# SwiGLU input projections with seven quarter-block products per pair of tiles

## The chip, the cores and the metric

The kernel runs on one core of a Trainium2 chip. The metric is the device time of one execution in microseconds (us); the profile gives the span of one profiled execution and, within it, every instruction.

## The reference

One inference step of a two-layer decoder trunk in float32, for 512 prompt tokens and 8 sample tokens that share the weights (520 columns in all, model width 1024). Layer 0 mixes tokens by a gated MLP over chunks, layer 1 by a gated delta rule. Each mixer is followed by the part that changes here:

```python
def rmsnorm(x, g):
    xf = x * lax.rsqrt(jnp.mean(x * x, axis=-1, keepdims=True) + EPS)
    return xf * g

def swiglu_ffn(h, w_in, w_out):
    gate, up = jnp.split(h @ w_in, 2, axis=-1)      # 1024 -> 2 x 2816
    return (jax.nn.silu(gate) * up) @ w_out         # 2816 -> 1024

x = x + swiglu_ffn(rmsnorm(x, norm_ffn[i]), ffn_w_in[i], ffn_w_out[i])
```

## The kernel before, in words

Activations lie with features on the 128 partitions: x is 8 tiles (k) of 128 features by 520 tokens. Every float32 product is made of three matmuls on rounded parts: weights and activations are split into a high part (a cast on ScalarE, `S`) and a low part (a subtraction on VectorE, `V`, or GpSimd, `G`), and `products` (L162) issues high x high, high x low and low x high for each k. `HALF` cuts the tokens in two, 256 and 264 columns; one half tile of output is 8 x 3 = 24 matmuls into one PSUM bank. Weights come from memory by SP's queue, 512 KB for an output tile (`load_raw`, L126), and are split by `split_w` (L133).

`ffn` (L418) runs over the 22 tiles of the inner width in chunks of 8, 8 and 6. For each tile it makes the gate product in two half tiles, multiplies it by the norm factor of each token (`norm.scaled`, L238), applies Silu, multiplies by the factor again on GpSimd (L430), makes the up product in two half tiles, multiplies (L436) and splits the result (`split_act`, L172) as input of the projection. Behind each chunk `out_proj` (L273) runs 8 tiles x 2 halves over it and adds to x. Its last `tail` tiles take first one half and then the other.

The norm does not hold up the products: `Feed` (L241) splits x times gain as soon as a tile of x is there, while `Norm` (L177) adds up squares. `finish` (L213) puts two steps behind later half tiles, by `after` (L148): `reduce` (column sums on TensorE, the reciprocal root in nine small VectorE operations, a diagonal) and `spread` (the factor brought to all partitions by TensorE, copied by ScalarE, L230).

The order is set by the program text, by pools of buffers (three raw weights, three split ones, three banks for products), and by a compile-time scheduler that may pull an instruction ahead where another waits; `pin` keeps some in program order. In layer 1 the new states of the samples (L1016) are laid between the products by `after`: a load, and three counts later one GpSimd operation of 128x512 (L1028) and four on VectorE (L1030).

## Time and profile before

| what | value |
|---|---|
| time, median of 3 runs | 1501.12 us (1499.31 to 1503.87) |
| profiled execution: span | 1499.8 us (no time around it is given) |
| instructions | 29605, of which 12192 matmuls |
| TensorE, weight loads | 97%, 95% busy |
| VectorE, ScalarE, GpSimd | 54%, 36%, 29% busy |
| moved by DMA | 155.69 MB, mean 104 GB/s |
| chain that ended last, by engine | PE 85%, DVE 11%, ACT 2% |

The chain is followed back from the last instruction: at each step to what released it, or to the instruction before it on its engine. A group of instructions is a line of the kernel with its operation and tiles (in and out, partitions x elements), its count, its total and mean time, and the idle time of the engine before it. PE is TensorE, PEld its weight loads, DVE VectorE, ACT ScalarE, POOL GpSimd, SP the engine whose queue issues the loads.

### The profile page before, as it was taken

Reading aid. Unit: us, or ns where it says so; the run is one execution under the profiler, and the core shown is the slowest. Engines: PE = TensorE matmul, PEld = TensorE weight load, DVE = VectorE, ACT = ScalarE, POOL = GpSimd, SP = SyncE. Lnnn points to the kernel's source line nnn. Section 1 sums busy time; section 2 is a strip of 40 time slices with the busy share of each in tenths; the row PEclk is TensorE's granted clock in tenths of the full one; section 3 lists DMA queues with packets and bytes.
Section 4 is the critical chain, followed back from the end, with each engine's and each line's share of the span. In section 5 each row is a group of like instructions: output and inputs, shape, how many; then the busy total and the mean of one; then the engine's idle time right before and its main releaser. Section 6 shows DMA issues by size and latency. Waiting matters only on the chain.

```text
span 1499.8 us, 29605 instructions
## 1 busy us (share of the span) xinstructions
PE 1447.5 (97%) x12192; PEld 1429.8 (95%) x12192; DVE 813.3 (54%) x1727; ACT 540.6 (36%) x1067; POOL 440.7 (29%) x468
## 2 busy tenths in 40 slices
PE   8999999999999999998788899999999999999997
PEld 8999999999999999998788888999999999999997
DVE  7447445553333333347777988686754344444344
ACT  5445323433312321334643255434433313321333
POOL 2113102333302320336444212311334412430333
PEclk9999999999999999999899999999999999999999
DMA  6222222322322232224311224234423443444331
GB/s 205 81 85 87 86 85 85 101 85 88 97 89 95 88 96 90 94 82 144 104 58 71 79 79 134 87 103 146 150 85 107 141 148 120 124 143 134 114 95 68
DMA packets 79367, 155.69 MB, mean 104 GB/s; under 512 B 10848, under 2 KB 41216, under 8 KB 79232
## 3 DMA queue, kind: packets, MB, share of 16 engines
q1 hardware_dynamic: 78944, 153.27, 31.1%
q8 instruction: 96, 1.57, 0.4%
q10 hardware_dynamic: 288, 0.52, 0.1%
q14 instruction: 39, 0.32, 0.1%
HBM read 142.18 MB, written 11.59 MB: 103 GB/s over the span
## 4 chain that ended last, share of the span: by engine, by line
PE 85%; DVE 11%; ACT 2%; issue 2%; DMA 1%; POOL 0%; SPq 0%; ACTq 0%; DVEq 0%; POOLq 0%
PE mm L168 76%; DVE kcs L579 1%; PE ax L406 1%; DVE sc L677 1%; DVE inv L678 1%; PE ax L867 1%; DVE t L579 1%; DVE sqacc L196 1%; PE ax L334 1%; DVE rs_u L118 1%; PE ax L643 1%; DVE inv L670 1%; PE sx L819 1%; PE sx L826 0%; PE ax L227 0%
## 5 line engine op out<-in xcount | busy, mean ns | idle before, releaser
L168 PE MATMUL mm<-hfh,wsp 128*128 128x256 f32 (+1 forms) x2816 | 510.4, 283 | 0.0
L168 PEld LDWEIGHTS mm<-hfh,wsp 128*128 128x128 f32 x2816 | 436.0, 189 | 0.1
L168 PE MATMUL mm<-hfl,wsp 128*128 128x256 f32 (+1 forms) x1408 | 398.8, 283 | 0.0
L138 ACT CAST wsp<-raw 128x1024 fp32r<-128x1024 f32 (+2 forms) x225 | 231.8, 1030 | 456.3 <-PE mm L168 408.5
L139 DVE TENSOR_TENSOR wsp<-raw,wsp 128x1024 fp32r<-128x1024 f32 (+2 forms) x193 | 234.0, 1213 | 91.4 <-ACT wsp L138 90.8
L168 PEld LDWEIGHTS mm<-hfl,wsp 128*128 128x128 f32 x1408 | 265.8, 189 | 0.0
L168 PE MATMUL mm<-fmh,wsp 128*128 128x264 f32 (+1 forms) x1408 | 254.9, 283 | 0.0
L168 PEld LDWEIGHTS mm<-fmh,wsp 128*128 128x128 f32 x1408 | 217.6, 188 | 0.0
L168 PE MATMUL mm<-hbh,wsp 128*128 128x264 f32 (+1 forms) x1024 | 203.9, 295 | 7.8 <-DVE t L574 5.7
L168 PE MATMUL mm<-hnh,wsp 128*128 128x264 f32 (+1 forms) x1024 | 197.9, 287 | 2.9 <-POOL wsp L139 1.0
L168 PE MATMUL mm<-fml,wsp 128*128 128x264 f32 (+1 forms) x704 | 198.9, 283 | 0.0
L430 POOL TENSOR_TENSOR t<-t,rbc 128x256 f32<-128x256 f32 x88 | 95.3, 1083 | 315.9 <-ACT t L429 315.9
L168 PEld LDWEIGHTS mm<-hbh,wsp 128*128 128x128 f32 x1024 | 166.8, 196 | 9.7 <-DVE t L574 6.3
L238 DVE TENSOR_TENSOR t<-mm,rbc 128x264 f32<-128x264 f32 (+1 forms) x160 | 68.4, 428 | 193.6 <-PE mm L168 192.1
L168 PEld LDWEIGHTS mm<-hnh,wsp 128*128 128x128 f32 x1024 | 161.5, 189 | 4.0 <-POOL wsp L139 1.2
L168 PE MATMUL mm<-hbl,wsp 128*128 128x264 f32 (+1 forms) x512 | 150.0, 293 | 0.0
L168 PE MATMUL mm<-hnl,wsp 128*128 128x256 f32 (+1 forms) x512 | 145.6, 285 | 0.4 <-DVE hnl L261 0.4
L175 POOL TENSOR_TENSOR fml<-t,fmh 128x256 fp32r<-128x256 f32 x88 | 95.9, 1089 | 150.0 <-ACT fmh L174 150.0
L168 PEld LDWEIGHTS mm<-fml,wsp 128*128 128x128 f32 x704 | 132.6, 188 | 0.0
L282 DVE TENSOR_TENSOR x<-mm,x 128x264 f32<-128x264 f32 (+1 forms) x128 | 54.5, 426 | 124.9 <-PE mm L168 124.5
L436 DVE TENSOR_TENSOR t<-mm,t 128x256 f32<-128x256 f32 x88 | 37.7, 429 | 119.2 <-PE mm L168 117.0
L168 PEld LDWEIGHTS mm<-hbl,wsp 128*128 128x128 f32 x512 | 100.3, 196 | 0.3
(331 smaller groups left out, 1989.9 us busy)
## 6 DMA issues: line engine op xcount, KB each, us to landing
raw<-in_f_w_in SPq DMA_DIRECT2D x88, 512.0 KB, 3.2
raw<-in_f_w_out SPq DMA_DIRECT2D x32, 512.0 KB, 3.5
raw<-in_b_w_in SPq DMA_DIRECT2D x32, 512.0 KB, 3.3
raw<-in_a_w_in SPq DMA_DIRECT2D x31, 512.0 KB, 3.2
raw<-in_a_w_out SPq DMA_DIRECT2D x16, 512.0 KB, 3.6
raw<-in_f_w_out SPq DMA_DIRECT2D x16, 384.0 KB, 3.1
L<-rows_d SPq DMA_DIRECT2D x16, 256.0 KB, 3.6
t<-in_st_delta SPq DMA_DIRECT2D x16, 256.0 KB, 3.2
```

Of the source, the lines that this page charges most:

```text
L118: V.tensor_tensor(u, u, s, ALU.mult)
L138: S.copy(hi, r)
L139: (eng or V).tensor_tensor(w[:, 1, i:i + n, :], r, hi.bitcast(F32), ALU.subtract)
L168: PE.matmul(ps[:, :n], lhsT=w[:, a, k, :], rhs=act[b][:, k, c0:c0 + n], start=(i == 0), stop=(i == last))
L175: (eng or G).tensor_tensor(act[1][:, k, c0:c0 + n], tmp, hi.bitcast(F32), ALU.subtract)
L196: (eng or G).tensor_tensor(a, a, t, ALU.add)
L238: V.tensor_tensor(t, ps[:, :n], self.r[:, c0:c0 + n], ALU.mult)
L282: V.tensor_tensor(dst, ps[:, :w], (xin(j)[:, c0:c0 + w] if xin else dst), ALU.add)
L334: PE.transpose(ps[:, j * P:(j + 1) * P], vf[j][:, c * C:(c + 1) * C], ident)
L430: G.tensor_tensor(s, s, norm.r[:, c0:c0 + nn], ALU.mult)
L436: V.tensor_tensor(sg[h], ps[:, :nn], sg[h], ALU.mult)
L579: V.scalar_tensor_tensor(y[:, :T], raw[:, j:j + T], wc[:, n, j:j + 1], y[:, :T], ALU.mult, ALU.add)
```

## The change

The input projections of SwiGLU are computed on blocks. An operand block is half of the features (4 tiles k) by half of the tokens (260 columns); a weight block is half of the features by one output tile, and two neighbouring output tiles make a two by two arrangement. Instead of eight products of blocks, seven are made, of sums and differences of blocks (`Seven`): the weight sums are four 128x512 operations on GpSimd for each pair of tiles (`load`), seven blocks of weights are split in four steps (`split`), and seven steps of 12 matmuls add into three banks; ScalarE copies intermediate sums out of PSUM, and VectorE combines them with the last ones (`step`). The activation sums are made once per layer (`quarter`). For this, activations are multiplied by gain and norm factor before they are split (`Scaled`), and the two multiplications behind the gate product go. The first pair of gate tiles and of up tiles in a layer is still made by half tiles; each later pair has one group of seven for gates and one for ups, their steps interleaved by the sorted list `plan` (one unit is one step of either). The projection of a chunk stands in that list too, and takes the other set of banks. Buffers: five raw weights and four split ones. The tail of `out_proj` grows from two tiles to three in both mixers' last projections and in layer 0's SwiGLU. The small weights of the next mixer are loaded at the end of layer 0's SwiGLU, not ahead of it; the samples' new states come every 10 counts, not 7, a count being a half tile or a step. The diff's core:

```diff
...
-    wraw = ctx.enter_context(tc.tile_pool(name="wraw", bufs=3))
-    wspl = ctx.enter_context(tc.tile_pool(name="wspl", bufs=3))
+    wraw = ctx.enter_context(tc.tile_pool(name="wraw", bufs=5))
+    wspl = ctx.enter_context(tc.tile_pool(name="wspl", bufs=4))
...
+        def finish(self, h, at=1, then=None):
+                if then:
+                    then()
...
+    class Scaled:
+        def __init__(self, x, gain, regions, sums, name):
+            self.x, self.gain, self.regions, self.sums, self.name = x, gain, regions, sums, name
+            self.act = None
+        def __call__(self, k, h, eng=None):
+            if self.act is None:
+                self.act = act_pair(*self.regions, self.name)
+                self.norm = Norm()
+            self.norm.add(self.x, k, h, V if k >= 6 else eng)
+            if k == KD - 1:
+                self.norm.finish(h, 1, lambda: self.half(h))
+        def half(self, h):
+            c0, n = HALF[h]
+            if not h:
+                self.work = region(7, [P, 4160], "work")
+            y = self.work.rearrange("p (k t) -> p k t", k=KD)
+            for k in range(KD):
+                a = y[:, k, c0:c0 + n]
+                V.scalar_tensor_tensor(a, self.x[:, k, c0:c0 + n], self.gain[:, k:k + 1], self.norm.r[:, c0:c0 + n], ALU.mult, ALU.mult)
+                split_act(a, self.act, k, c0, n, G if k % 2 else V)
+            if h:
+                self.q = tuple(region(i, [P, 4, HK, HT], self.name + "q", F32R) for i in self.sums)
+                after(2, lambda: self.quarter(y, 0))
+                after(3, lambda: self.quarter(y, 2))
+        def quarter(self, y, k):
+            def of(k0, h):
+                return y[:, k0 + k:k0 + k + 2, h * HT:(h + 1) * HT]
+            def two():
+                return t2()[:, :2 * HT].rearrange("p (k t) -> p k t", k=2)
+            def put(i, t, eng):
+                hi = self.q[0][:, i, k:k + 2, :]
+                S.copy(hi, t)
+                eng.tensor_tensor(self.q[1][:, i, k:k + 2, :], t, hi.bitcast(F32), ALU.subtract)
+            s1, s2, s3, s4 = two(), two(), two(), two()
+            V.tensor_tensor(s1, of(0, 1), of(HK, 1), ALU.subtract)
+            V.tensor_tensor(s2, s1, of(0, 0), ALU.subtract)
+            G.tensor_tensor(s3, of(0, 0), of(0, 1), ALU.subtract)
+            V.tensor_tensor(s4, s2, of(HK, 0), ALU.add)
+            for i, (t, eng) in enumerate(((s1, V), (s2, G), (s3, V), (s4, G))):
+                put(i, t, eng)
+        def operand(self, i, b, k):
+            plain = {0: (0, 0), 3: (HK, 0), 6: (HK, 1)}
+            if i in plain:
+                k0, h = plain[i]
+                return self.act[b][:, k0 + k, h * HT:(h + 1) * HT]
+            return self.q[b][:, {1: 0, 2: 1, 4: 2, 5: 3}[i], k, :]
+    class Seven:
+        def __init__(self, feed, src, bank, done, slot):
+            self.feed, self.src, self.bank, self.take, self.slot = feed, src, bank, done, slot
+            self.w, self.banks = {}, {}
+        def load(self):
+            f = self.feed
+            self.raw = [load_raw(a, KD) for a in self.src]
+            o = 2048 * self.slot
+            b11, b21 = (self.raw[0][:, k:k + HK, :] for k in (0, HK))
+            b12, b22 = (self.raw[1][:, k:k + HK, :] for k in (0, HK))
+            t = [f.work[:, o + 512 * i:o + 512 * i + 512].rearrange("p (k n) -> p k n", k=HK) for i in range(4)]
+            G.tensor_tensor(t[0], b11, b12, ALU.add)
+            G.tensor_tensor(t[1], t[0], b22, ALU.add)
+            G.tensor_tensor(t[2], b12, b22, ALU.add)
+            G.tensor_tensor(t[3], t[1], b21, ALU.add)
+            self.parts = (b11, t[0], t[1], b21, t[2], b22, t[3])
+        def split(self, j):
+            w = wspl.tile([P, 2, 2, HK, P], F32R, tag="wsp", name=nm("wsp"))
+            for e, i in enumerate(range(2 * j, min(2 * j + 2, 7))):
+                r, hi = self.parts[i], w[:, 0, e]
+                S.copy(hi, r)
+                V.tensor_tensor(w[:, 1, e], r, hi.bitcast(F32), ALU.subtract)
+                self.w[i] = (w[:, 0, e], w[:, 1, e])
+        def step(self, i):
+            fresh, at = i in (0, 1, 3), "acabaca"[i]
+            if fresh:
+                self.banks[at] = self.bank()
+            ps = self.banks[at]
+            if i == 0:
+                self.kept = t2()
+            w = self.w.pop(i)
+            n, last = 0, 3 * HK - 1
+            for k in range(HK):
+                for a, b in ((0, 0), (0, 1), (1, 0)):
+                    PE.matmul(ps[:, :HT], lhsT=w[a][:, k, :], rhs=self.feed.operand(i, b, k), start=fresh and n == 0, stop=n == last, skip_group_check=not fresh)
+                    n += 1
+            if i == 0:
+                S.copy(self.kept[:, :HT], ps[:, :HT])
+            elif i == 1:
+                S.copy(self.kept[:, HT:TT], ps[:, :HT])
+            elif i == 2:
+                self.kept2 = t1()[:, :HT]
+                S.copy(self.kept2, ps[:, :HT])
+            elif i == 3:
+                self.take(0, 0, lambda t: V.tensor_tensor(t, ps[:, :HT], self.kept[:, :HT], ALU.add))
+            elif i == 4:
+                self.take(1, 1, lambda t: V.tensor_tensor(t, self.kept[:, HT:TT], ps[:, :HT], ALU.subtract))
+            elif i == 5:
+                self.take(1, 0, lambda t: V.tensor_tensor(t, ps[:, :HT], self.kept2, ALU.subtract))
+            else:
+                self.take(0, 1, None, ps[:, :HT])
+            tick()
-    def out_proj(w_out, k0, nk, act, x, xin=None, then=None, early=((), ()), halves=(0, 1), tail=2):
+    def out_proj(w_out, k0, nk, act, x, xin=None, then=None, early=((), ()), halves=(0, 1), tail=2, bank=None):
-            ps = mm3(ws[j], nk, act, h) if h or j not in first else first[j]
+            ps = mm3(ws[j], nk, act, h, bank) if h or j not in first else first[j]
...
-    feed = Feed(x, gffn[:, 0], (1, 2), "hf")
+    feed = Scaled(x, gffn[:, 0], (1, 2), (5, 6), "hf")
...
-        out_proj(a_w_out, half * 8, 8, mid, x, then=feed if half else None)
-    def ffn(layer, x, feed, then):
+        out_proj(a_w_out, half * 8, 8, mid, x, then=feed if half else None, tail=2 + half)
+    def ffn(layer, x, feed, then, final=None):
+        mids = {}
+        def mid(n):
+            c = n // 8
+            if c not in mids:
+                mids[c] = act_pair(3, 4, "fm")
+            return mids[c]
+        hf = feed.act
+        sg = [t2(), t2()]
+        ws = [weights(w_in[n]) for n in (0, 1)]
+        ups = []
+        for h in range(2):
+            c0, nn = HALF[h]
+            for j in range(2):
+                ps = mm3(ws[j], KD, hf, h)
+                S.activation(sg[j][:, c0:c0 + nn], ps[:, :nn], AF.Silu)
+            for j in range(2):
+                if not h:
+                    ups.append(weights(w_in[NF + j]))
+                ps = mm3(ups[j], KD, hf, h)
+                t = t1()[:, :nn]
+                V.tensor_tensor(t, ps[:, :nn], sg[j][:, c0:c0 + nn], ALU.mult)
+                split_act(t, mid(0), j, c0, nn)
+        def project(c):
+            k0, nk = 8 * c, min(8, NF - 8 * c)
+            end = k0 + nk == NF
+            if end and final:
+                final()
+            out_proj(w_out, k0, nk, mids[c], x, then=then if end else None, halves=(layer, 1 - layer), tail=3, bank=None if end else axps)
+        plan = []
+        for p in range(NF // 2 - 1):
+            n = 2 * p + 2
+            gates = {}
+            def gate(j, h, get, ps=None, gates=gates):
+                if not gates:
+                    gates.update({0: t2(), 1: t2()})
+                g = gates[j][:, h * HT:(h + 1) * HT]
+                if get:
+                    get(g)
+                S.activation(g, g if get else ps, AF.Silu)
+            def up(j, h, get, ps=None, gates=gates, n=n):
+                g, t = gates[j][:, h * HT:(h + 1) * HT], t1()[:, :HT]
+                if get:
+                    get(t)
+                    V.tensor_tensor(t, t, g, ALU.mult)
+                else:
+                    V.tensor_tensor(t, ps, g, ALU.mult)
+                split_act(t, mid(n + j), (n + j) % 8, h * HT, HT)
+            for q, (o, bank, take) in enumerate(((0, mmps, gate), (NF, axps, up))):
+                at = 14 * p + 7 * q
+                seven = Seven(feed, [w_in[o + n + j] for j in range(2)], bank, take, q)
+                plan.append((at - 6.2, seven.load))
+                for j in range(4):
+                    plan.append((at + 4 * j - 4.5, lambda seven=seven, j=j: seven.split(j)))
+                for i in range(7):
+                    plan.append((at + 2 * i, lambda seven=seven, i=i: seven.step(i)))
+            if n % 8 == 6 or n + 2 == NF:
+                plan.append((14 * p + (20.2 if n + 2 < NF else 20), lambda c=n // 8: project(c)))
+        for _, event in sorted(plan, key=lambda e: e[0]):
+            event()
...
+    wbas = []
+    def load_ba():
+        wba = region(5, [P, 2, 8, P], "wba", F32R)
+        rba = region(6, [P, 8, 16], "rba")
+        G.memset(wba.bitcast(F32), 0.0)
+        nc.sync.dma_start(rba, b_w_ba)
+        S.copy(wba[:, 0, :, 0:16], rba)
+        V.tensor_tensor(wba[:, 1, :, 0:16], rba, wba[:, 0, :, 0:16].bitcast(F32), ALU.subtract)
+        wbas.append(wba)
+    ffn(0, x, feed, feed_b, load_ba)
+    wba = wbas[0]
...
-    feed = Feed(x, gffn[:, 1], (5, 6), "hf")
-    out_proj(b_w_out, 0, 8, ob, x, xin=xin, then=feed, early=(wo, first))
+    feed = Scaled(x, gffn[:, 1], (5, 6), (1, 2), "hf")
+    out_proj(b_w_out, 0, 8, ob, x, xin=xin, then=feed, early=(wo, first), tail=3)
...
-            new_states(hd, i, 10 + 7 * (2 * hd + i))
+            new_states(hd, i, 12 + 10 * (2 * hd + i))
...
-    nc = _bacc.Bacc("TRN2", target_bir_lowering=False, num_devices=1)
+    nc = _bacc.Bacc("TRN2", target_bir_lowering=False, num_devices=1, dynamic_dma_scratch_size=64)
...
```

## Rows read from the trace of the kernel before

**Rows 1.** The page's parts 1 and 2: engines over the span, TensorE in 40 slices

```profile
PE 1447.5 (97%) x12192; PEld 1429.8 (95%) x12192; DVE 813.3 (54%) x1727; ACT 540.6 (36%) x1067; POOL 440.7 (29%) x468
PE   8999999999999999998788899999999999999997
```

**Rows 2.** The chain that ended last, window 300 to 720 us: start, us, what

```profile
324.98 365.84 PE mm L168 x3048
```

**Rows 3.** TensorE's timeline at layer 0's SwiGLU; its waits from 1060 us on

```profile
317.13 0.68 PE L227 MATMUL ax<-t,ones 128*128 128x128 f32 x4 [1.94 <-DVE t L221]
...
PE ax L227 <- DVE t L221: 1.9, 1, 1.9
```

**Rows 4.** GpSimd: L1028 alone (ns min/median/max), then groups by shape

```profile
L1028 POOL TENSOR_TENSOR sc<-sc,smb x16: 1043/1050/1578, 1144.3 to 1445.3; 128x512 f32<-128x512 f32 x16
...
L430 POOL TENSOR_TENSOR t<-t,rbc 128x264 f32<-128x264 f32 x44 | 62.9, 1430 | 109.5 <-ACT t L429 109.5
L430 POOL TENSOR_TENSOR t<-t,rbc 128x256 f32<-128x256 f32 x44 | 32.4, 736 | 206.4 <-ACT t L429 206.4
```

**Rows 5.** VectorE's groups by shape

```profile
L139 DVE TENSOR_TENSOR wsp<-raw,wsp 128x1024 fp32r<-128x1024 f32 x179 | 221.2, 1236 | 85.6 <-ACT wsp L138 85.1
L436 DVE TENSOR_TENSOR t<-mm,t 128x264 f32<-128x264 f32 x44 | 19.0, 432 | 95.0 <-PE mm L168 95.0
...
L413 DVE TENSOR_TENSOR t<-t,t 128x264 f32<-128x264 f32 x16 | 6.8, 427 | 0.0
L940 DVE TENSOR_TENSOR obl<-t,obh 128x512 fp32r<-128x512 f32 x8 | 5.4, 684 | 0.3 <-ACT obh L939 0.3
```

**Rows 6.** ScalarE's groups by shape

```profile
L138 ACT CAST wsp<-raw 128x1024 fp32r<-128x1024 f32 x207 | 217.2, 1049 | 436.5 <-PE mm L168 396.3 <-issue 31.7 <-ACT t L192 3.6
...
L174 ACT CAST fmh<-t 128x264 fp32r<-128x264 f32 x44 | 18.0, 408 | 0.9 <-DVE t L436 0.9
...
L939 ACT CAST obh<-t 128x512 fp32r<-128x512 f32 x8 | 4.9, 618 | 13.3 <-DVE t L937 13.3
...
L230 ACT COPY rbc<-ax 128x264 f32<-128x264 f32 x5 | 1.9, 378 | 13.7 <-PE ax L227 13.7
```

**Rows 7.** Timelines of VectorE, then GpSimd, 270 to 325 us

```profile
277.20 0.49 DVE L261 SCALAR_TENSOR_TENSOR hfl<-x,gffn,hfh 128x264 fp32r<-128x264 f32 x1
...
293.32 2.33 DVE L261 SCALAR_TENSOR_TENSOR hfl<-x,gffn,hfh 128x264 fp32r<-128x264 f32 x1 [1.11 <-ACT hfh L260]
295.57 0.41 DVE L282 TENSOR_TENSOR x<-mm,x 128x256 f32<-128x256 f32 x1
...
308.07 0.48 DVE L261 SCALAR_TENSOR_TENSOR hfl<-x,gffn,hfh 128x256 fp32r<-128x256 f32 x1 [0.58 <-ACT hfh L260]
308.48 0.42 DVE L196 TENSOR_TENSOR sqacc<-sqacc,t 128x256 f32<-128x256 f32 x1
...
313.01 2.39 DVE L118 TENSOR_TENSOR rs_u<-rs_u,nrm_s 128x3 f32<-128x3 f32 x1
...
292.95 2.40 POOL L139 TENSOR_TENSOR wsp<-raw,wsp 128x1024 fp32r<-128x1024 f32 x1 [1.61 <-ACT wsp L138]
295.30 0.95 POOL L196 TENSOR_TENSOR sqacc<-sqacc,t 128x264 f32<-128x264 f32 x1
```

**Rows 8.** VectorE, line L238: count, ns min/median/max

```profile
L238 DVE TENSOR_TENSOR t<-mm,rbc x160: 403/426/434, 44.6 to 1447.5; 128x256 f32<-128x256 f32 x80, 128x264 f32<-128x264 f32 x80
```

**Rows 9.** VectorE's timeline in layer 1, one new state

```profile
1185.73 1.14 DVE L1030 SCALAR_TENSOR_TENSOR sc<-sc,kqs,sc 128x128 f32<-128x128 f32 x4 [1.66 <-POOL sc L1028]
```

**Rows 10.** VectorE's timeline, second root of layer 0, first and last operation

```profile
321.16 0.16 DVE L208 TENSOR_SCALAR nrm_s<-ax 128x2 f32<-128x2 f32 x1 [1.41 <-PE ax L205]
...
323.19 0.61 DVE L221 TENSOR_SCALAR t<-ident,rs_y 128x128 f32<-128x128 f32 x3
```

**Rows 11.** The page's part 6, DMA issues

```profile
raw<-in_f_w_in SPq DMA_DIRECT2D x88, 512.0 KB, 3.2
```

**Rows 12.** Stretches: us, busy of PE, PEld, DVE, ACT, POOL (x), clock, DMA

```profile
1125.00:1210.00 85.00, 85.00 (x711) 85.00 (x710) 35.76 (x62) 24.57 (x42) 35.08 (x32) 1.00 0.40 125
```

More of the change, by code (lines that the diff above doesn't have):

```diff
@@ L150, in after, with tick @@
         steps.setdefault(done[0] + n, []).append(step)
-    def mm3(w, nk, act, h):
-        ps = products(w, nk, act, h)
+    def tick():
         done[0] += 1
@@ L156, in mm3 @@
             step()
+    def mm3(w, nk, act, h, bank=None):
+        ps = products(w, nk, act, h, bank)
+        tick()
         return ps
@@ L160, in pin, with products @@
         tc.keep_in_program_order(ins)
-    def products(w, nk, act, h):
+    def products(w, nk, act, h, bank=None):
         c0, n = HALF[h]
-        ps = mmps()
+        ps = (bank or mmps)()
         i, last = 0, 3 * nk - 1
@@ L414, in trunk @@
                 split_act(m[:, :nn], mid, k, c0, nn)
-        out_proj(a_w_out, half * 8, 8, mid, x, then=feed if half else None)
-    def ffn(layer, x, feed, then):
+        out_proj(a_w_out, half * 8, 8, mid, x, then=feed if half else None, tail=2 + half)
+    def ffn(layer, x, feed, then, final=None):
         w_in, w_out = f_w_in[layer], f_w_out[layer]
-        hf, norm = feed.act, feed.norm
-        for c0f, nk in ((0, 8), (8, 8), (16, 6)):
-            mid = act_pair(3, 4, "fm")
-            for k in range(nk):
-                wg = weights(w_in[c0f + k], eng=G if c0f + k == 0 else V)
-                sg = []
-                for h in range(2):
-                    c0, nn = HALF[h]
-                    s = norm.scaled(mm3(wg, KD, hf, h), h)
-                    S.activation(s, s, AF.Silu)
-                    G.tensor_tensor(s, s, norm.r[:, c0:c0 + nn], ALU.mult)
-                    sg.append(s)
-                wu = weights(w_in[NF + c0f + k], eng=G if c0f + k == 0 else V)
-                for h in range(2):
-                    c0, nn = HALF[h]
-                    ps = mm3(wu, KD, hf, h)
-                    V.tensor_tensor(sg[h], ps[:, :nn], sg[h], ALU.mult)
-                    split_act(sg[h], mid, k, c0, nn)
-            out_proj(w_out, c0f, nk, mid, x, then=then if c0f == 16 else None, halves=(layer, 1 - layer), tail=2 + layer)
```

11 lines of the change are left out of this document (3 added, 8 removed).

## The prediction

> **What bounds the kernel now.** I read the page's busy times first, then the chain of waits, then the waits of each engine. TensorE is busy 97% of the span, and in the 40 slices it falls below nine tenths only at the start, around the middle mixer and at the end [rows 1]. The chain shows why no other engine matters in the SwiGLU stages: from 324.98 us on it consists of 3048 matmuls in 365.84 us and nothing else, 0.120 us each [rows 2]. So there a matmul that goes away is worth 0.120 us, as long as whatever replaces it stays hidden. TensorE waits only at the two entrances of SwiGLU, 1.9 us each, for the small multiplications behind the norm factor [rows 3]. ScalarE and GpSimd are free for two thirds of the span or so and VectorE for almost half, but that is an average; the question is what they can do together inside the changed stretch.
>
> The profiled execution has a span of 1499.8 us; the page gives no time around it. That is 1.3 us under the median 1501.1 of the runs, whose own spread is 4.6. I count changes against the span and put the result beside the median. Below 0.3% (4.5 us) a measurement of this kernel can't tell a change from none.
>
> **Matmuls removed.** A pair of output tiles took 2 x 2 half tiles of 24 matmuls, 96. It now takes seven products of 4 x 3 matmuls of 260 columns, 84. The first pair of gates and of ups in each layer stays as it was; the other 10 pairs of each go in 40 groups of seven: 40 x 12 = 480 matmuls. The 0.120 us is the mean of 256 and 264 columns, and 260 lies between: **-57.6 us**. Per pair of groups (one of gates, one of ups, interleaved) TensorE needs 168 x 0.120 = 20.2 us where it needed 23.0.
>
> The Trainium skill (TensorE: Matmul & The Clock Gate, section Back-to-back issue gap) gives N/2.4 + 2.5 ns for a warm matmul alone, 110.8 ns at 260 columns; an estimate from it would make the saving 53.2 us. The rows' 120 ns is larger, so the measurement decides.
>
> **What a pair of groups costs the other engines.** GpSimd: eight sums of weight blocks, 128x512. The nearest operation of this shape takes 1.05 us in the median; the four low parts of activations take 0.74 each when undisturbed [rows 4]. Sum 8 x 1.05 + 4 x 0.74 = 11.4 us; the multiplication by the norm factor on GpSimd (88 operations, 95 us in all [rows 4]) goes. VectorE: 14 low parts of weights at 0.684 (128x512), seven reads of PSUM at 0.43, three products in SBUF at 0.43: 9.6 + 3.0 + 1.3 = 13.9 us [rows 5]. ScalarE: 14 casts at 0.62, six copies out of PSUM at 0.38, four casts at 0.41 and four Silu taken as these: 14.3 us [rows 6]. Each alone fits under 20.2, with ScalarE and VectorE at 70%.
>
> **The shared resource.** VectorE and GpSimd do not run side by side when VectorE reads two operands in SBUF. At 292.95 GpSimd starts an operation of 2.40 us, and a VectorE operation that starts 0.37 later takes 2.33 in place of 0.49, ending 0.30 behind it; then GpSimd's next one ends 0.60 behind VectorE. A VectorE operation that reads PSUM passes in 0.41 meanwhile. Even the three-column step of the reciprocal root waits 2.39 [rows 7]. VectorE's reads of PSUM are never lengthened: 434 ns at most in 160 [rows 8]. So what matters is the sum of both engines' time on the shared path. With fixed parts overlapped, a VectorE operation holds it for about its columns over 0.95 per ns (0.30 at 264), and GpSimd 0.14 less than its own time: 14 x 0.56 + 3 x 0.30 + 8 x 0.91 + 4 x 0.60 = **18.4 us** of 20.2. With nothing overlapped it is 9.6 + 1.3 + 11.4 = **22.3 us**. The two ends lie on either side of TensorE's 20.2. Split weights are asked for 4.5 steps ahead of use (6.5 us, a step being 1.44), so a delay of 2 to 3 us is absorbed, and the projection between chunks (16 x 24 x 0.12 = 46 us, almost without GpSimd) lets a backlog drain. I am nearer to the tight end, since in rows 7 both engines hand over without a gap, and take 0.5 us of stall per pair of groups in layer 0: **+5 us** (bounds 0 to 33).
>
> In layer 1 the new states of the samples run in between, now every 10 counts, about 1.4 per pair of groups: each 1.05 on GpSimd [rows 4] and 1.14 on VectorE for four [rows 9], both on the shared path, +2.7 to 3.1 us. That gives 21 to 25 against 20.2. I take 1.5 us of stall per pair: **+15 us** (bounds 0 to 62).
>
> The Trainium skill (GPSIMD Engine Reference, section 4.1 Engine selection) sends two-input elementwise work to VectorE and calls GpSimd about 2x slower. Here 1.05 stands against 0.684, 1.5x; at the page's 2x a block sum would be 1.37 us, by estimate, and the shared path 24.8 with nothing overlapped, more than the 23.0 of before. The measured 1.05 decides, and the change then stays on the right side.
>
> **The entrance.** Before, products started on x times gain while the norm factor was still being made. Now each half waits for it. With T the end of the last first-half product of the mixer's projection (whose tail grows from two tiles to three): x, square and sum about T+1.5; the column sums go behind the next half tile, T+2.9; root and diagonal take 2.6 us [rows 10], T+5.9; the spread stands behind the second, and the factor is in SBUF at T+6.8. Then VectorE scales eight tiles (0.41 each, back to back [rows 7]), subtracts four low parts and GpSimd four (0.60 each on the shared path), beside two evacuations: 7 to 8 us, so T+14.5, when TensorE is free at T+9.2. The first tile takes in k by k, and would have ended at T+12.1: about 3 us of stall. The second half has two more tiles of cover: 0.5. Then the quarter sums: ten operations of 520 columns on VectorE and six on GpSimd, about 12 us on the shared path; the weight sums of the first group use the same region and queue behind the last read of it on GpSimd. TensorE has 12 us of first-pair products to cover it: I take 2. Sum 5.5 per layer, **+11 us** (bounds 2 to 24); the two waits of 1.9 that stood there go into the longer tail: **-3.8**.
>
> **Smaller edits.** Splits for the next groups hold two of the four buffers while the projection of a chunk runs, but its tail wants three, so two products must move ahead of it; the bound is 0 to 2.7 us (a cast and a subtraction, 1.05 + 1.24 and handovers [rows 5]) at four places; I take 0.5: +2. At the last chunk the final low part on GpSimd is needed about 1.8 us after its product: 1 us each: +2. Loads: the same blocks, 3.2 us to landing [rows 11], asked for two at a time over five buffers and thus several steps ahead on SP's queue; if that cover went, 3 us per pair. The moved memset and load of the small weights have 35 us of projection over them: nothing; uncovered they would cost some 4 us once.
>
> **Sum:** -57.6 + 5 + 15 + 11 - 3.8 + 4 = -26.4, so 1473.4 for the span and **1474.7** beside the median.
>
> **Rivals.** (a) TensorE paces everything: the shared path stays at its tight 18.4, and even new states are absorbed by the projections. For it: GpSimd and VectorE together are busy 71 of 85 us in the stretch of layer 1 already, without a TensorE wait [rows 12]. -57.6 + 2 to 11 - 3.8 + 2: 1444 to 1453. Chance 0.10. (b) The shared path paces: 1.5 us of stall in layer 0 and 3.2 in layer 1 per pair, 47 in all: -57.6 + 47 + 11 - 3.8 + 4 = +0.6, 1490 to 1508. For it: the untightened 22.3 and the ScalarE queue, which waits in order for GpSimd's sums and holds up evacuations. Chance 0.18. (c) Slower: VectorE waits out a GpSimd operation at almost every turn, as in [rows 7]. A pair then costs VectorE's own 13.9 plus GpSimd's held 9.7, 23.6 us, and 26.5 in layer 1; 3.4 x 10 + 6.3 x 10 = 97, less about 4 us per chunk that slack takes up (24): +73. -57.6 + 73 + 11.2 = +27: 1528 (1508 to 1545). It decides from about 2.3 us of stall per pair, where the sum crosses zero. Against it: VectorE's reads of PSUM, a fifth of its time, overlap with GpSimd. Chance 0.17.
>
> The Trainium skill (SBUF — State Buffer, section SBUF: two separate sides) says that the loser of this pair blocks for the whole instruction. That is the mechanism of (c), and rows 7 agree (2.33 us in place of 0.49); it gives no rate for the hand-over.
>
> That fewer products run than stated is no rival: the counts are fixed by the loops.
>
> **How the numbers follow.** Forecast 0.55, 1453 to 1490, centre 1474.7. Faster by over 0.3%: 0.55 + 0.10 + 0.08 of (b). Within 0.3%: 0.08. Slower: 0.17 + 0.02. The range reaches over (b) and most of (a): 1447 to 1508, leaving out (c) and a little of (a).
>
> **What would show it.** Matmuls 480 fewer, at 0.120 us apart. GpSimd's block sums at 1.05 alone and near 1.6 behind VectorE; the weight subtractions spread from 0.68 to 1.6. TensorE idle before products of group steps, released by VectorE's weight parts, few in layer 0, more in layer 1; and 3 to 6 us at each entrance, released by the scaled activations. It is wrong if TensorE waits for evacuations or loads, if the entrances cost over 12 us each, or if layer 0 stalls as much as layer 1.

## The result and the profile after

The changed kernel takes 1555.41 us (median of 4 runs, 1554.48 to 1557.60) where the kernel before took 1502.43 on the same chip: a ratio of 1.0363 (95% interval 1.0345 to 1.0382). It is slower by 53 us, against a forecast of 26 us faster. The profiled execution of it has a span of 1553.6 us, 53.8 more than before.

The page's part 1 (busy time, share, instructions) and the first line of its part 4 (the chain that ended last, by engine) show that the matmuls did go and that TensorE now waits:

```profile
PE 1427.6 (92%) x11712; PEld 1392.4 (90%) x11712; DVE 1050.3 (68%) x1999; ACT 648.9 (42%) x1402; POOL 590.2 (38%) x564
...
PE 55%; DVE 30%; ACT 6%; issue 5%; POOL 3%; DMA 1%; SPq 0%; ACTq 0%; DVEq 0%; POOLq 0%
```

There are 480 matmuls fewer than in [rows 1], as counted. But TensorE falls from 97% to 92% of the span, and the chain's share of VectorE rises from 11% to 30%. Stage by stage, from first matmuls on the timeline: SwiGLU of layer 0 lasts 411.6 us (before 396.7), the second mixer 392.7 (389.2), SwiGLU of layer 1 to the end 433.3 (396.3), the start 1.5 less; in all +53.8. The two SwiGLU stages also lost 57.6 us of matmuls, so some 110 us of new waiting came in.

TensorE's waits (total us, times, longest), from the second down; the first lies in the second mixer (L808, 20.0 us, before 14.2):

```profile
...
PE mm L375 <- DVE t L567: 14.7, 2, 7.3
PE ax L173 <- ACT wsp L140: 14.1, 8, 2.7
PE ax L375 <- DVE wsp L361: 10.2, 4, 4.6
PE mm L375 <- ACT t L378: 9.0, 2, 4.5
PE mm L375 <- DVE t L387: 8.7, 8, 2.0
PE ax L232 <- DVE t L226: 6.3, 3, 4.1
```

L567 is the reading of a bank of the first, plain pair of tiles; L378 and L387 are reads of a group's banks; L361 is a group's weight part on VectorE; L140 is the split of a projection's first weight. None of these waits is on a load. The two 1.9 us waits of [rows 3] are gone.

By stretches (us, busy of PE, PEld, DVE, ACT, POOL with counts, granted clock, DMA): the entrance of layer 0, its later groups, and two stretches of groups of layer 1.

```profile
345.00:380.00 35.00, 22.89 (x159) 22.18 (x159) 30.75 (x30) 15.51 (x33) 29.41 (x20) 0.76 0.20 62
...
472.00:563.00 91.00, 88.61 (x725) 87.14 (x724) 73.11 (x93) 44.58 (x103) 53.87 (x42) 1.00 0.29 93
...
1185.00:1241.00 56.00, 48.71 (x383) 47.46 (x382) 44.45 (x67) 25.30 (x61) 35.73 (x30) 0.97 0.46 136
1290.00:1390.00 100.00, 89.43 (x698) 87.05 (x698) 76.55 (x112) 44.94 (x104) 58.50 (x47) 0.97 0.41 121
```

In layer 0 the later groups lose 2.4 us of 91; in layer 1, where the new states run too, 7.3 of 56 and 10.6 of 100. At the entrance TensorE works 22.9 us of 35 while VectorE and GpSimd are both near full. The timelines of VectorE, then GpSimd there (start, us), show how full:

```profile
347.11 1.77 DVE L317 TENSOR_TENSOR hfq<-t,hfq 128x520 fp32r<-128x520 f32 x1
348.80 1.76 DVE L323 TENSOR_TENSOR t<-t,work 128x520 f32<-128x520 f32 x1
350.49 1.76 DVE L317 TENSOR_TENSOR hfq<-t,hfq 128x520 fp32r<-128x520 f32 x1
352.17 1.75 DVE L361 TENSOR_TENSOR wsp<-work,wsp 128x512 fp32r<-128x512 f32 x1
353.84 0.42 DVE L567 TENSOR_TENSOR t<-mm,t 128x264 f32<-128x264 f32 x1
...
348.40 1.60 POOL L350 TENSOR_TENSOR work<-raw,raw 128x512 f32<-128x512 f32 x1
349.97 1.72 POOL L352 TENSOR_TENSOR work<-raw 128x512 f32<-128x512 f32 x1
351.65 1.72 POOL L353 TENSOR_TENSOR work<-work,raw 128x512 f32<-128x512 f32 x1
```

Both engines advance by one operation every 1.69 us, in turn. The product that this L567 reads, the first up tile's second half, was finished at 342.1; its read, behind the quarter sums in VectorE's queue, starts at 353.84, and TensorE stands 7.3 us for that bank. A further 4.5 us (L378) follow in the same way. From within the first gap on the clock is granted at its lower level, 1.2 GHz, for 17 us. Layer 1 shows the same gaps, 7.34 and 4.49.

### The profile page after: what moved, and what is told of

It is laid out like the page before. It is cut to its first block, busy times and chain, and to the rows that moved or that the text cites. A ratio compares the mean times of both kernels' runs of the same rounds, so it can differ in the third digit from the quotient of the medians.

```text
span 1553.6 us, 29290 instructions
## 1 busy us (share of the span) xinstructions
PE 1427.6 (92%) x11712; PEld 1392.4 (90%) x11712; DVE 1050.3 (68%) x1999; ACT 648.9 (42%) x1402; POOL 590.2 (38%) x564
## 4 chain that ended last, share of the span: by engine, by line
PE 55%; DVE 30%; ACT 6%; issue 5%; POOL 3%; DMA 1%; SPq 0%; ACTq 0%; DVEq 0%; POOLq 0%
PE mm L173 28%; PE ax L173 12%; DVE wsp L361 10%; PE mm L375 4%; PE ax L375 4%; DVE t L595 2%; ACT wsp L360 1%; DVE kcs L758 1%; DVE work L300 1%; ACT wsp L140 1%; DVE sc L1209 1%; PE ax L530 1%; DVE t L758 1%; DVE inv L857 1%; PE ax L1046 1%
## 5 line engine op out<-in xcount | busy, mean ns | idle before, releaser
L140 ACT CAST wsp<-raw 128x1024 fp32r<-128x1024 f32 (+2 forms) x145 | 147.6, 1018 | 264.0 <-PE mm L173 125.9
L173 PE MATMUL ax<-fmh,wsp 128*128 128x256 f32 (+1 forms) x1024 | 191.0, 287 | 14.8 <-ACT wsp L140 14.1
L173 PEld LDWEIGHTS ax<-fmh,wsp 128*128 128x128 f32 x1024 | 161.4, 192 | 17.7 <-ACT wsp L140 15.8
L141 DVE TENSOR_TENSOR wsp<-raw,wsp 128x1024 fp32r<-128x1024 f32 (+2 forms) x117 | 141.8, 1212 | 47.8 <-ACT wsp L140 47.3
L361 DVE TENSOR_TENSOR wsp<-work,wsp 128x512 fp32r<-128x512 f32 x160 | 155.9, 974 | 16.1 <-ACT wsp L360 15.9
L375 PE MATMUL mm<-hfq,wsp 128*128 128x260 f32 x960 | 138.0, 295 | 27.0 <-DVE t L567 14.7
L375 PEld LDWEIGHTS mm<-hfq,wsp 128*128 128x128 f32 x960 | 128.7, 200 | 29.2 <-DVE t L567 15.1
L361 DVE TENSOR_TENSOR wsp<-raw,wsp 128x512 fp32r<-128x512 f32 x120 | 122.7, 1024 | 35.2 <-ACT wsp L360 35.2
L173 PE MATMUL ax<-fml,wsp 128*128 128x264 f32 (+1 forms) x512 | 146.0, 286 | 0.0
L375 PE MATMUL ax<-hfq,wsp 128*128 128x260 f32 x960 | 128.3, 284 | 3.7 <-ACT t L378 2.6
L375 PEld LDWEIGHTS ax<-hfq,wsp 128*128 128x128 f32 x960 | 120.3, 188 | 5.6 <-ACT t L378 4.1
L375 PE MATMUL ax<-hfh,wsp 128*128 128x260 f32 x480 | 99.9, 290 | 10.6 <-DVE wsp L361 10.2
L375 PE MATMUL mm<-hfh,wsp 128*128 128x260 f32 x480 | 100.4, 291 | 9.3 <-DVE t L387 8.7
```

Source lines behind the costliest of these rows:

```text
L140: S.copy(hi, r)
L141: (eng or V).tensor_tensor(w[:, 1, i:i + n, :], r, hi.bitcast(F32), ALU.subtract)
L173: PE.matmul(ps[:, :n], lhsT=w[:, a, k, :], rhs=act[b][:, k, c0:c0 + n], start=(i == 0), stop=(i == last))
L361: V.tensor_tensor(w[:, 1, e], r, hi.bitcast(F32), ALU.subtract)
L375: PE.matmul(ps[:, :HT], lhsT=w[a][:, k, :], rhs=self.feed.operand(i, b, k), start=fresh and n == 0, stop=n == last, skip_group_check=not f ...
```

## The experiments

Theory S: in the new stages VectorE's operations with two operands in SBUF and GpSimd's operations exclude each other, so the times for which they hold the path add up and set the end. Each time below is that of one run unless a range stands with it; "before" is the kernel before on the same chip, and as that took 1502.0 to 1507.0 on the chips used, a few us between two runs say nothing.

**GpSimd's weight sums left out.**

```diff
-            G.tensor_tensor(t[0], b11, b12, ALU.add)
...
-            self.parts = (b11, t[0], t[1], b21, t[2], b22, t[3])
+            self.parts = (b11, b12, b22, b21, b12, b22, b21)
```

> The four sums of weight blocks of each group are left out (raw blocks stand in their place), so GpSimd has 160 operations of 128x512 less; everything else is as in the changed kernel (1555.4 us). Theory S (VectorE and GpSimd hold up each other on the path that they share): the stretch of layer 1's groups loses most of its 33 us of waits, each entrance about half of its 19, so 45 us less (30 to 60), near 1510. Rival B (buffers and banks of the groups hold TensorE up, whatever GpSimd does): less than 10 us change.

Measured 1487.76 (before 1506.98): 68 us less than the changed kernel, more than S had given, and the largest effect of all. In its groups VectorE's operations (count, busy, mean ns) are back near their quiet times:

```profile
L356 DVE TENSOR_TENSOR wsp<-raw,wsp 128x512 fp32r<-128x512 f32 x280 | 195.3, 721 | 85.4 <-ACT wsp L355 85.1
...
L590 DVE TENSOR_TENSOR t<-t,t 128x260 f32<-128x260 f32 x60 | 25.5, 426 | 0.8
L1204 DVE SCALAR_TENSOR_TENSOR sc<-sc,kqs,sc 128x128 f32<-128x128 f32 x64 | 20.4, 377 | 31.6 <-POOL sc L1202 15.5 <-DMA sc<-dl_d 12.1 <-issue 4.0
```

The same groups in the changed kernel:

```profile
L361 DVE TENSOR_TENSOR wsp<-work,wsp 128x512 fp32r<-128x512 f32 x160 | 155.9, 974 | 16.1 <-ACT wsp L360 15.9
...
L361 DVE TENSOR_TENSOR wsp<-raw,wsp 128x512 fp32r<-128x512 f32 x120 | 122.7, 1024 | 35.2 <-ACT wsp L360 35.2
L595 DVE TENSOR_TENSOR t<-t,t 128x260 f32<-128x260 f32 x60 | 48.0, 800 | 0.7
...
L1209 DVE SCALAR_TENSOR_TENSOR sc<-sc,kqs,sc 128x128 f32<-128x128 f32 x64 | 35.4, 604 | 36.6 <-POOL sc L1207 29.0 <-DMA sc<-dl_d 7.6
```

So the sums hold up VectorE: 721 becomes 974 and 1024 ns, 426 becomes 800. As four of the seven splits of a group also no longer wait for a sum here, this run alone doesn't show which of the two makes the 68 us.

**The sums of activations left out; the new states left out.**

```diff
...
-                after(2, lambda: self.quarter(y, 0))
-                after(3, lambda: self.quarter(y, 2))
+                pass
...
-            return self.q[b][:, {1: 0, 2: 1, 4: 2, 5: 3}[i], k, :]
+            return self.act[b][:, k, 0:HT]
```

```diff
-            new_states(hd, i, 12 + 10 * (2 * hd + i))
+            pass
```

> The sums of activation blocks are left out (plain blocks are multiplied in their place): 20 operations on VectorE, 12 on GpSimd and 16 on ScalarE less in the changed kernel's two entrances, the normalisation ahead of the products stays. Theory S: each entrance falls from about 19 us lost to about 6, so 26 us less in all (18 to 32), near 1529. Rival N (the normalisation itself is what the entrance costs): less than 8 us change.

> The new states of the samples are left out in layer 1 (their outputs are not written): 16 operations of 128x512 on GpSimd and 64 of 128x128 on VectorE less, with their loads and stores. Theory S: layer 1's groups, which lose 33 us against 5 in layer 0, fall to the level of layer 0: 20 to 28 us less, near 1531. Rival: layer 1 is slow for another reason (its loads, its buffers in other regions), under 8 us.

Measured 1535.62 and 1527.40: 20 and 28 us less, within what S gave. Without the states the stage of layer 1 falls from 433.3 to 403.2 us.

**Two other causes of the waits.** First the up products of the plain pair take the other set of banks; then idle matmuls keep TensorE at work in the two gaps of each entrance.

```diff
-                ps = mm3(ups[j], KD, hf, h)
+                ps = mm3(ups[j], KD, hf, h, axps)
```

> The first pair's up products go to the other set of banks, so that the first group of seven no longer waits for a bank which VectorE's multiplication L567 must read out first (the wait of 7.3 us that the profile names at each entrance). Theory S: the same wait appears behind VectorE's weight and activation parts, as these are late for the same reason: change under 6 us. Rival B: 7 us per entrance and the slow clock behind them go, 20 to 30 us less, near 1530.

```diff
...
+                for _ in range(dummy):
+                    pin(PE.matmul(pd[:, :HT], lhsT=self.feed.act[0][:, 0, :P], rhs=self.feed.act[0][:, 0, :HT], start=True, stop=True))
...
```

> In front of steps 1 and 2 of each layer's first group stand 54 and 34 products whose result nobody reads, in the places where TensorE waits 7.3 and 4.5 us; nothing else is changed. Theory C (the 17 us that the clock stays at its lower level behind these waits cost 8 us per layer by themselves): the clock stays up and 10 to 16 us go, near 1542. Rival (VectorE and GpSimd set the end of this stretch whatever the clock): under 4 us.

Measured 1556.96 and 1557.77, no gain from either. With the other banks the wait moves to VectorE's weight parts (L361, 17.0 us in all), as S had it. With the idle matmuls the row of the entrance has the full clock, 88 of its 262 matmuls being the idle ones; but the first projection still starts 115.2 us after the stage's first matmul, to the tenth as in the changed kernel. VectorE and GpSimd, 33.2 and 31.4 of 35 us busy, set the end:

```profile
345.00:380.00 35.00, 31.84 (x262) 31.22 (x261) 33.19 (x29) 15.74 (x35) 31.40 (x20) 1.00 0.19 61
```

The low clock behind the gap is thus a consequence and costs next to nothing of its own.

**Two plain pairs, quarter sums later; eight products throughout.**

```diff
-                after(2, lambda: self.quarter(y, 0))
-                after(3, lambda: self.quarter(y, 2))
+                after(4, lambda: self.quarter(y, 0))
+                after(7, lambda: self.quarter(y, 2))
...
+        for q in range(2):
...
-        for p in range(NF // 2 - 1):
-            n = 2 * p + 2
+        for p in range(NF // 2 - 2):
+            n = 2 * p + 4
```

This is the edit of the first run. The second makes all eleven pairs of a layer in that loop and leaves the quarter sums out.

> Two pairs of gate and up tiles, not one, are made by half tiles at the start of each layer, and the two halves of the activation sums are put behind later products (4 and 7 counts in place of 2 and 3). 24 matmuls more per layer (+2.9 us each, +5.8). Theory S: VectorE and GpSimd need some 27 us of shared path at the entrance where TensorE has 17 us of products; with 23 us more of them the wait and the slow clock go, 15 to 17 us per layer, net 24 to 29 us less, near 1529. Rival B: the first group stalls as before, wherever it stands: 6 us more.

> The changed kernel without groups of seven: all pairs of tiles by half tiles, eight products, but normalised ahead of the products, in the changed kernel's order of pairs, with its buffers, tails and banks. States come every 7 counts, since there are fewer counts. Theory S: about the time of before, 1496 to 1508, the entrance costs at most 3 us per layer. Rival N: 15 us or more per layer is lost at the entrance, 1530 or more.

Two plain pairs give 1535.06, 20 us less, though 48 matmuls come back; the 7.3 and 4.5 us gaps are gone. Eight products on activations normalised beforehand give 1514.38 (before 1506.98), 7 us slower than before, 6 above what was expected: about 4 us of that lie at layer 0's entrance (97.7 us to the projection, before 93.8). Normalising beforehand has a price of its own.

**Buffers for the projections.**

```diff
-    wraw = ctx.enter_context(tc.tile_pool(name="wraw", bufs=5))
-    wspl = ctx.enter_context(tc.tile_pool(name="wspl", bufs=4))
+    wraw = ctx.enter_context(tc.tile_pool(name="wraw", bufs=4))
+    wspl = ctx.enter_context(tc.tile_pool(name="wspl", bufs=5))
...
-    t2p = ctx.enter_context(tc.tile_pool(name="t2p", bufs=6))
+    t2p = ctx.enter_context(tc.tile_pool(name="t2p", bufs=5))
...
-    sc = ctx.enter_context(tc.tile_pool(name="sc", bufs=3))
+    sc = ctx.enter_context(tc.tile_pool(name="sc", bufs=2))
```

> The changed kernel with five buffers of split weights in place of four, so that the split of the first tile of a projection between the chunks need not wait until the tile groups before it have given one back (room for it from the raw weights, 5 to 4 buffers, the tiles of 520, 6 to 5, and the small tiles of the states, 3 to 2; nothing that is computed changes). Theory W (each of the four projections between chunks loses 4 to 6 us because its first split weight comes late for want of a buffer, TensorE idle 2.65 us there and at half the clock behind it): those waits go, about 16 to 20 us, 1537 (1530 to 1545). Rival Q (the buffer is free in time, but VectorE and ScalarE have other work queued ahead of the split, so another buffer changes little): under 6 us, 1549 to 1558.

Measured 1568.43, slower by 13: both expectations missed. The wait for L140 does leave the list (half of it is now one on L141), but the reads of banks by ScalarE (L378) come later everywhere:

```profile
PE mm L375 <- ACT t L378: 18.8, 12, 4.5
PE mm L375 <- DVE t L567: 18.1, 2, 9.1
PE mm L375 <- DVE t L387: 15.6, 6, 3.5
...
PE ax L173 <- DVE wsp L141: 6.8, 4, 2.5
```

A fifth buffer doesn't fit in SBUF beside the rest. Room for it was taken from others (four raw weights, five tiles of 520, two of the states), so this run doesn't settle what the projections' wait is worth.

**The states moved into the projections.**

```diff
-            new_states(hd, i, 12 + 10 * (2 * hd + i))
...
+    def some_states():
+        for m in range(5):
+            new_states(*todo.pop(0), 1 + int(2.5 * m))
+    new_states(*todo.pop(0), 4)
...
+            if states:
+                states()
             out_proj(w_out, k0, nk, mids[c], x, then=then if end else None, halves=(layer, 1 - layer), tail=3, bank=None if end else axps)
```

> The changed kernel with the new states of layer 1 (sixteen tiles, each a few operations of VectorE on pairs of operands in SBUF) laid into the three projections, five in each and one early, in place of one every ten ticks through the groups of tiles. Theory S (in the groups VectorE and GpSimd share one path to SBUF and every VectorE operation with two operands there lengthens a group; in a projection that path has room): most of the 28 us that leaving the states out saved, about 22 us, 1533 (1525 to 1541). Rival (the states cost what they cost wherever they stand, since the projections are short of VectorE too): within 6 us of the changed kernel, 1549 to 1561.

Measured 1536.54, 19 us less, as S had it. From the first matmul of layer 1's first projection to that of its second, four pairs of groups further on, it takes 136.1 us in place of 149.3.

**Subtractions taken from PSUM.** The direct test of S: the same subtraction, but one operand lies in PSUM.

```diff
                 S.copy(hi, r)
+                if e == 0:
+                    p = sxps().rearrange("p (k n) -> p k n", k=HK)
+                    S.copy(p, r)
+                    r = p
                 V.tensor_tensor(w[:, 1, e], r, hi.bitcast(F32), ALU.subtract)
```

> The changed kernel in which, for four of the seven parts of a tile group, ScalarE also copies the block to a bank of PSUM and VectorE subtracts from that copy, so that only one operand of that subtraction lies in SBUF (160 of the 280 subtractions; the same numbers, and ScalarE has 160 copies of 512 columns more, some 0.6 us each). Theory S (a VectorE operation with both operands in SBUF and a GpSimd operation keep each other out): those 160 take about 0.7 us in place of 0.97 to 1.02 and no longer hold up GpSimd's sums; the GpSimd sums come down toward their quiet 1.05 us, and the time falls by 10 to 25 us, 1530 to 1545. Rival (GpSimd is slow for its own reasons, or VectorE's count of operations sets the end): GpSimd's sums stay at 1.3 to 1.6 us and the time is not lower, 1553 to 1575 with ScalarE's added work.

> The changed kernel with all seven subtractions of a tile group taken from a copy in PSUM (280 of 280, where the run before had 160). Theory S: the 120 that still had both operands in SBUF come from 1.0 to 0.7 us, another 8 to 15 us, 1518 to 1526. Rival (with 280 copies more ScalarE, or the two banks the copies go through, set the end): 1533 or more, ScalarE late at the take-over of the products.

Measured 1533.37 with 160 of 280 and 1521.49 with all (the condition `True`): 22 and 34 us less, though ScalarE has 160 and 280 copies more. Line L365 with 160, by operands, and then with all (ns min/median/max):

```profile
L365 DVE TENSOR_TENSOR wsp<-sx,wsp 128x512 fp32r<-128x512 f32 x160 | 109.6, 685 | 74.4 <-ACT wsp L360 72.5 <-PE mm L379 1.5
L365 DVE TENSOR_TENSOR wsp<-raw,wsp 128x512 fp32r<-128x512 f32 x80 | 79.6, 995 | 0.8
```

```profile
L365 DVE TENSOR_TENSOR wsp<-sx,wsp x280: 675/692/694, 343.2 to 1465.8; 128x512 fp32r<-128x512 f32 x140
...
L351 POOL TENSOR_TENSOR work<-work,raw x40: 1275/1298/1636, 341.0 to 1443.4; 128x512 f32<-128x512 f32 x40
```

From PSUM none of 280 takes over 0.694 us; with both operands in SBUF the longest in the changed kernel took 1.859. In the changed kernel the same line of GpSimd is held up in 25 of its 40 operations, which take over 1.4 us:

```profile
L351 POOL TENSOR_TENSOR work<-work,raw x40: 1261/1616/1734, 341.6 to 1479.9; 128x512 f32<-128x512 f32 x40
```

One part of the expectation failed: GpSimd's sums don't come down toward 1.05. Undisturbed, they take 1.30.

**Things put together.** The edits shown so far, and for the last versions the whole first chunk (four pairs) made of plain products, its projection behind them:

```diff
-                after(2, lambda: self.quarter(y, 0))
-                after(3, lambda: self.quarter(y, 2))
+                after(10, lambda: self.quarter(y, 0))
+                after(18, lambda: self.quarter(y, 2))
...
+        for q in range(4):
...
+            if q % 4 == 3:
+                project(q // 4)
...
-        for p in range(NF // 2 - 1):
-            n = 2 * p + 2
+        for p in range(NF // 2 - 4):
+            n = 2 * p + 8
```

> The changed kernel with three of its losses taken away together: two plain pairs of tiles ahead of the groups with the quarter sums at ticks 4 and 7 (20 us on its own, but 48 of 480 group steps fewer), five buffers of split weights, and layer 1's new states in the projections. If the losses are separate places (theory S with W): the savings add up, some 55 us, 1500 (1490 to 1512), no more than level with the kernel before. Rival (they are one and the same wait, which moves from place to place): 1520 to 1535.

> The changed kernel with the three things that helped on their own: two plain pairs ahead of the groups with the quarter sums at ticks 4 and 7 (20 us on its own), layer 1's new states in the projections (19 us), and four of seven subtractions from PSUM (22 us). Buffers as in the changed kernel. If each took time from a place of its own (entrance; groups of layer 1; groups of both layers): up to 61 us, 1495; the last two meet in the groups of layer 1, so 1500 (1492 to 1512). Rival (the three are one and the same shortage of VectorE and GpSimd, and TensorE is the bound as soon as one is lifted): 1515 to 1530.

> As the run with the three things together, but the whole first chunk of a layer (four pairs) plain, the quarter sums at ticks 10 and 18: 4 of the 20 pairs per kernel fewer are products of quarters than there (14 of 20 rather than 18). By TensorE alone 4 times 2.88 = 11.5 us more than that run; if the groups are still held by VectorE and GpSimd, a group pair of quarters and a plain pair take about the same, and it is within 5 us of that run. Expected 1500 to 1512.

With the five buffers: 1520.24, at the lower edge of the rival's range; after what those buffers did alone this doesn't tell the theories apart. With the buffers left as they were and 144 of 252 subtractions from PSUM: 1497.65 (before 1502.00), so 58 of 61 us add up: three separate places. With the whole first chunk plain: 1490.36, better than expected, although that makes 96 matmuls more: two more plain pairs in each layer, with the quarter sums later still, cost less than they freed.

> The same kernel as the run with the first chunk plain, three relieved, timed in rounds against the kernel before: 1490 (1487 to 1494), a ratio of 0.992 to before.

> The run with the first chunk plain, with all seven subtractions of a group taken from PSUM in place of four (196 in place of 112). If VectorE and GpSimd still hold the groups: 3 to 8 us less than that run's 1490, 1482 to 1488. If TensorE paces them by now (95 per cent busy there): within 3 us of it, 1487 to 1494.

> Eight products throughout on activations normalised beforehand (the run at 1514), with layer 1's new states in the projections. It tells whether the products of quarters have a part in what is gained, or only the place of the states. If the states were held up by GpSimd's sums alone, moving them does nothing where there are no sums: 1508 to 1516, and the products of quarters are worth some 20 us. Rival (the states are better placed in the projections whatever the products): 1495 or less, and the quarters are worth little.

In four runs the version with the first chunk plain takes 1491.24 (1490.89 to 1492.12) against 1503.30, a ratio of 0.9921 (0.9902 to 0.9939): 0.8% under the kernel before. Layer 0's plain pairs, and then its first projection with the groups of the second chunk behind it:

```profile
345.00:380.00 35.00, 35.00 (x296) 35.00 (x295) 20.24 (x21) 13.73 (x26) 16.61 (x13) 1.00 0.28 91
...
413.00:555.00 142.00, 141.96 (x1181) 141.58 (x1181) 87.94 (x132) 84.43 (x171) 74.08 (x58) 1.00 0.30 97
```

TensorE is without a gap there. All subtractions from PSUM then give nothing more, 1492.48 (1491.89 to 1494.14), as is to be expected where TensorE paces. Still, the version has 336 matmuls fewer than the kernel before, 40 us by count, and gains 12: SwiGLU of layer 0 is 9.8 us shorter than before and that of layer 1 2.2, where the count gives 20 for each. Eight products with the states moved take 1525.46, 11 more than without the move and 9 above what the first theory gave; why the move costs the plain version time stays open. So the states' place alone is not the gain: against the better of the two plain versions on normalised activations the products of quarters, with what was done to relieve them, are worth some 20 us (23 by the times, 19 when each is set against the kernel before on its chip). Subtractions from PSUM were not tried in a plain version.

## Why the prediction was wrong

The likeliest case failed. What came is the mechanism of rival (c), VectorE and GpSimd waiting for each other, but beyond its range and mostly not where (c) had put it. Against the sum, the entrances cost 31 us more, the projections between chunks 17 and layer 1's states 15. Behind these stand a block sum that was priced too low and one-time work that was left without a price. Two of the prediction's own signs of being wrong appear, waits for evacuations and entrances of over 12 us each.

**Right.** The matmuls: 480 fewer, at 63.00 us for 521 in an undisturbed stretch (610 to 673 us), 0.121 each, so -58 where -57.6 was counted. The waits of [rows 3] went. The stall in layer 0's groups: idle 0.6, 2.4 and 0.1 us in three stretches, 3 against 5. The last low parts, 2.1 against 2. Loads set no wait.

**The step that failed first: the price of a block sum.** "The nearest operation of this shape takes 1.05 us in the median." That operation multiplies by a factor repeated along 128 columns; a block sum reads two full tiles. It takes 1.30 us undisturbed. The trace of before had a row of just this kind, which the prediction doesn't use: L770, two full tiles of 128x512.

```profile
L770 POOL TENSOR_TENSOR q<-q,t x8: 1270/1296/1691, 913.3 to 985.6; 128x512 f32<-128x512 f32 x8
```

With 1.30 the shared path is 14 x 0.56 + 0.9 + 8 x 1.16 + 2.4 = 20.4 us tight and 9.6 + 1.3 + 8 x 1.30 + 3.0 = 24.3 with nothing overlapped: no end lies clearly under TensorE's 20.2, and the loose one is over the 23.0 of before.

The Trainium skill (GPSIMD Engine Reference, section 3.1) measures 1.96x between GpSimd and VectorE for an add of two float32 tiles; 1.30 against 0.684 is 1.9x. The prediction had set the 2x that the same reference gives in section 4.1 aside for 1.05; here the page was the better guide, as far as the ratio goes.

**The tight end of the sharing held.** "I am nearer to the tight end, since in rows 7 both engines hand over without a gap." They do, and a pair of turns takes 1.69 us. By the prediction's own rule, with 1.30, it is 0.56 + 1.16 = 1.72; with the 0.91 that was taken for GpSimd it would be 1.47. So the overlap was right and only the price in it wrong. The sum of both engines' own quiet times, 0.68 + 1.30, is 0.3 us too much, and the 24.3 that it gives per pair would mean some 41 us of stall in layer 0's ten pairs, where 3 were idle in the groups and 11 at the projections.

The Trainium skill (SBUF — State Buffer, section SBUF: two separate sides) has the pair exclude each other when VectorE has two inputs in SBUF. The runs with a PSUM operand agree: 0.69 us at most.

**The entrances: +11 for both, measured about 42.** In layer 0, 7.3 + 4.5 idle, half of 17.1 us at the lower clock, 1.5 of small waits: 22 us; in layer 1, 7.3 + 4.5, half of 13.6 and as many small waits: 20. The small waits are those for the scaled activations, for which 3.5 us were taken. What failed is the step behind them: "TensorE has 12 us of first-pair products to cover it: I take 2" priced the quarter sums alone, at the tight rate. It named the first group's weight sums without a price, and left out that group's splits and the reads of the plain pair's banks, which stand behind all of these in VectorE's queue. The quarter sums are the smaller part: without them it is 107.8 and 116.2 us from a layer's first matmul to its first projection, with them 115.2 and 125.1, before 93.8 and 95.3. The prediction names a wait for such reads as a sign that it is wrong, but put no price on it. Since keeping the clock up gained nothing, the halves of the slow stretches count as the time in which VectorE and GpSimd were still behind.

**The projections between chunks: +2, measured about 19.** 2.65 + 1.13 us of wait at each in layer 0 and 2.13 + 1.14 in layer 1, and behind all but the last of the four 1.7 at the lower clock (half of 3.4): 5.5 twice, 5.0 and 3.3. The bound of 2.7 counted the tail's split alone. The backlog of the groups, which the projection was to absorb, seems to be paid here instead: with subtractions from PSUM the wait on L140 falls from 14.1 to 8.8 us (160 of 280) and 7.3 (all), and in the version with the first chunk plain TensorE enters the first projection, behind plain pairs, without a gap, with as many buffers of split weights. What part the buffers have remains open.

**Layer 1's states: stall +15, measured about 30.** 22.9 us idle in three stretches and half of 13.6 at the lower clock. Leaving the states out gives 28 us back, moving them 19. They went onto a path that had no room left: the tight sum with 1.30 and the states is 23.1 to 23.5 us a pair, 2.9 to 3.3 over TensorE's 20.2, or 29 to 33 in ten pairs. This agreement was found afterwards and no run was made to test it.

**The rest.** The ends of the stages take about 5 us where 2 were allowed: the last low parts as allowed, and some 3 in the norm behind layer 0's SwiGLU, with a wait of 4.1 (L226). The second mixer takes 3.6. Of 111 us that came in, these terms name some 102; the rest lies in waits too small for me to place.

**The rivals.** (c) had the mechanism, but as a price of the groups: it gave 97 us there before slack. Measured, the groups lost some 33 and the places around them 61. (a), TensorE paces everything, is what the relieved version reaches in the stretches shown. (b)'s 3.2 us a pair in layer 1 is near the measured 3.0, but it took the entrances over from the forecast.

## What to carry to other kernels

Price an operation by a row that reads its operands in the same way (full tiles or repeated ones, SBUF or PSUM), not by the nearest shape; and where two engines exclude each other, add the times for which they hold the path and compare that sum with the bound in every stage, at the entrance first, where the new one-time work meets the steady work and each piece of it wants a price. Where the sum was too large here, an operand in PSUM, a later start behind more plain products and another stage for the side work gave 34, 20 and 19 us.

## What was not expected of the hardware

VectorE subtracts 128x512 from PSUM in 0.69 us beside a busy GpSimd without one exception in 280, while the same subtraction with both operands in SBUF takes up to 1.86. Two engines in turn keep up a steady 1.69 us per pair for some 20 us on end, about 0.3 less than their quiet times together. GpSimd takes 1.05 us for 128x512 with a repeated factor (medians of 1.04 to 1.05 in four lines of the trace of before: L631, L811, L836, L1028) and 1.30 for two full tiles. And TensorE at its lower clock behind a wait cost nothing that shows where another engine set the end: 1557.8 us with the clock kept up, 1555.4 without.
